# A fourth raw weight buffer in the input projections of a hybrid encoder block

## The chip, the core and the metric

The kernel runs on one core of a Trainium2 chip. The core has five engines with an instruction queue each, every one of them worked off in order: TensorE (PE in the profile, with its weight loads as PEld), VectorE (DVE), ScalarE (ACT), GpSimd (POOL) and SyncE (SP), which here issues the transfers of the weights. The metric is device time in microseconds (us) for one execution; less is better.

## The reference

One block over a sequence of 256 positions and 2048 channels, all in float32. The part that matters here is the first stage:

```python
proj = jnp.einsum('bsd,dc->bsc', h, w_in)            # 2048 -> 12800 columns
lru_x, conv_x, conv_bg, conv_cg, g_lru, g_conv = jnp.split(proj, SPLIT_POINTS, axis=-1)
u = centred_dwconv(lru_x, lru_conv_w, lru_conv_b, LRU_CONV_LEFT)
h_fwd = rg_lru_direction(u, lru_w_a[0], lru_b_a[0], lru_w_x[0], ..., False)   # 20 heads of 128
h_bwd = rg_lru_direction(u, lru_w_a[1], lru_b_a[1], lru_w_x[1], ..., True)
y_lru = jnp.einsum('bsw,wd->bsd', h_fwd + h_bwd, w_lru_out)
v = centred_dwconv(conv_cg * conv_x, sc_conv_w, sc_conv_b, SHORT_CONV_LEFT)
y_conv = jnp.einsum('bsc,cd->bsd', conv_bg * v, w_conv_out)
merged = jax.nn.sigmoid(g_lru) * y_lru + jax.nn.sigmoid(g_conv) * y_conv
h = layer_norm(ALPHA * h + jnp.einsum('bsd,de->bse', merged, w_o), ln1_g, ln1_b)
ff = jnp.square(jax.nn.relu(jnp.einsum('bsd,df->bsf', h, mlp_w1) + mlp_b1))
h = layer_norm(ALPHA * h + jnp.einsum('bsf,fd->bsd', ff, mlp_w2) + mlp_b2, ln2_g, ln2_b)
```

In `rg_lru_direction` each head's `u` goes through two 128x128 gates (sigmoid), and the gates drive a linear recurrence along the sequence (exp, tanh, square root, scan).

## The kernel before

**Precision.** Every operand of a product is kept as a high part and a low part: `hi` is the value cast to the matmul's type, `lo` what the cast left over. For each weight tile `raw` (128 partitions x 1024 values, 512 KB) SP issues the transfer, ACT makes `hi` (L66), DVE makes `lo` (L67). Then PE multiplies: for each of the tile's eight 128x128 blocks one matmul of `hi` with both halves of the input (512 columns, L137) and one of `lo` with the high half (256 columns, L138).

**The stream of weights.** Class `Weights` holds one list of tiles for the whole kernel, in the order in which PE needs them. `load` (L82) takes the next entry: buffers, a transfer, the split. `take` gives a tile to PE's code and makes the loads run five tiles ahead (`AHEAD`). Each kind of buffer is a ring in the pool `wp`: 3 buffers `raw`, 6 `hi`, 6 `lo`. A transfer into a `raw` buffer must wait until DVE has made the `lo` of the tile that had the buffer before, which is the last reader; a cast into a `hi` buffer must wait until PE is done with the tile six places earlier.

**The stages.** In order: the input projections (the tiles below); the 32 gate blocks `sg`; the two output products `yl` and `yc`; `o` with the first norm; the two halves of the MLP, `f` and `d`. The input projections' stage reads 156 tiles: 8 of `b` (the first four column blocks together), then in rounds by head h from 1 to 19: the two tiles of `l{h}` (the recurrent branch's columns), one half-size tile `g{h-1}` (the gate weights of the head before), and two or three `c` blocks of the convolution branch, of two tiles each; then `g19`. This makes 38 tiles of `l`, 90 of `c` and 20 of `g`.

**What comes behind each block.** After an `l` block, `lru_post` adds the two halves of the PSUM bank (`t_l` on ACT, L234; `pad` on DVE, L237), makes the short convolution `u` (four DVE steps, L277 and L279) and splits it into `us` (ACT L66, DVE L67), which the gate's matmuls read (L298 to L300). After the gate, ACT makes four sigmoids (L306). After each second head `recur` handles two heads together: exp and tanh on ACT (L323, L324), products on POOL and DVE (L328, L329), square roots on ACT (L333), scans on DVE (L338, L339); ACT loads another table of functions between them. This burst comes nine times inside the stage.

**What sets the order.** The program is written in job order; a scheduler then sets the order of each engine's queue from priorities and from what it estimates to be ready, with the buffers' waits counted in. So the number of buffers can move instructions. The recurrent branch has a pool of its own, `lp` (L255), open from the start until the first `sg` block is read out; a pool for the gates' results is then opened in its place.

Of the kernel before, what the change touches and what calls it, by code (L numbers as in the profile page):

```python
# [8 lines left out]
F32 = mybir.dt.float32  # L9
# [5 lines left out]
P = 128  # L15
# [11 lines left out]
CH = 8  # L27
# [20 lines left out]
def block_kernel(ctx: ExitStack, tc: tile.TileContext, xT, x, par, w_first, w_in, w_gate, w_lru, w_conv, w_o, w1, w2,  # L48
# [3 lines left out]
    wp = ctx.enter_context(tc.tile_pool(name="wp", bufs=1))  # L52
# [17 lines left out]
    class Weights:  # L70
# [3 lines left out]
            self.specs, self.tiles, self.taken = [], [], 0  # L74

        def alloc(self, name):
            raw = wp.tile([P, CH * P], F32, tag="raw", name=f"raw_{name}", bufs=3)
            hi = wp.tile([P, CH * P], F32R, tag="hi", name=f"hi_{name}", bufs=BUFS)
            lo = wp.tile([P, CH * P], F32R, tag="lo", name=f"lo_{name}", bufs=BUFS)
            return raw, hi, lo  # L80
# [161 lines left out]
    def open_pool(name):  # L242
        scope[name] = es = ExitStack()
        return es.enter_context(tc.tile_pool(name=name, bufs=1, reuse_waits="tile"))
# [10 lines left out]
    lp = open_pool("lru")  # L255
# [337 lines left out]
    src, n, name = stream.specs[0]  # L593
    raw, hi, lo = stream.alloc(name)
# [77 lines left out]
```

## Time and profile before

| | |
|---|---|
| runs | 1645.41 us median of 3 (1641.05 to 1648.22) |
| the profiled execution | 1647.63 us, of which the span from the first to the last instruction is 1645.6 us |
| mean granted TensorE clock | 0.994 |
| PE busy, of the span | 98% |
| DVE, ACT, POOL busy | 64%, 52%, 4% |
| input projections' stage | from the start to 432.9 us, the first `sg` matmul |
| transfers | 312.05 MB, 190 GB/s over the span |

Busy time of PE counts every matmul from its start to its modelled end, and neighbours overlap. So small stops of PE are better found from the starts of successive matmuls, and from the idle time that the profile prints with the instruction that came late, than from the busy share. In the trace's lists of instructions the columns are: start, duration (us), engine, line, operation, what it writes and reads, how many; and in brackets the idle time of the engine before it and what ended that.

### The profile page before, as it was taken

What the parts mean: (1) busy time and instruction counts of PE and PEld (TensorE: products, weight loads), DVE (VectorE), ACT (ScalarE), POOL (GpSimd) and SP (SyncE); (2) the same over time, 40 slices, a digit from 0 to 9 for tenths busy, and PEclk for the clock granted to TensorE, in tenths of its full rate; (3) what the DMA queues carried; (4) which work ended last, traced back from release to release, by engine and by line L of the source; (5) the groups of instructions that cost most, each with busy time, mean ns of one, the idle gap of its engine ahead of it and who ended that gap; (6) DMA issues with size and microseconds to landing.
All of it is one profiled execution on the core that took longest, in us unless ns stands there. A gap on an engine that the chain in (4) does not pass through costs nothing.

```text
span 1645.6 us, 22702 instructions
## 1 busy us (share of the span) xinstructions
PE 1616.0 (98%) x8592; PEld 1377.5 (84%) x8592; DVE 1060.3 (64%) x1435; ACT 849.1 (52%) x1216; POOL 62.2 (4%) x69
## 2 busy tenths in 40 slices
PE   8999999999999999999999899999999999999997
PEld 7888888888888888888888788888888888888885
DVE  6788898888865546666555687654444666655444
ACT  5777676677755444444343545543333444543331
POOL 0111111111100000000000000000000000000001
PEclk9999999999999999999999899999999999999999
DMA  7555555555565555655774455555555555565552
GB/s 252 169 179 192 181 178 186 186 170 189 186 206 205 191 177 188 190 188 185 249 257 159 152 188 203 189 186 190 186 186 190 187 186 191 188 235 192 184 186 102
DMA packets 88364, 312.05 MB, mean 190 GB/s; under 512 B 9792, under 2 KB 10176, under 8 KB 87360
## 3 DMA queue, kind: packets, MB, share of 16 engines
q1 hardware_dynamic: 86976, 302.75, 54.9%
q0 software_dynamic: 992, 7.34, 1.2%
q8 instruction: 67, 1.10, 0.3%
q10 hardware_dynamic: 288, 0.52, 0.1%
q14 instruction: 41, 0.34, 0.1%
HBM read 308.48 MB, written 2.10 MB: 189 GB/s over the span
## 4 chain that ended last, share of the span: by engine, by line
PE 80%; DVE 6%; DMA 6%; ACT 4%; issue 3%; POOL 0%; SPq 0%; POOLq 0%; ACTq 0%; DVEq 0%
PE ps_f L137 15%; PE ps_f L138 7%; PE pr_d L208 7%; PE pr_d L206 7%; PE pr_d L207 7%; PE ps_sg L137 7%; PE ps_yl L137 5%; PE ps_sg L138 4%; PE ps_yc L137 4%; PE ps_c L137 4%; DMA raw_l<-in_w_in 2%; PE ps_yl L138 2%; DMA raw_c<-in_w_in 2%; PE ps_c L138 2%; PE ps_yc L138 2%
## 5 line engine op out<-in xcount | busy, mean ns | idle before, releaser
L137 PE MATMUL ps_f<-hsp,hi_f 128*128 128x512 f32 x1024 | 360.6, 395 | 0.9 <-DVE hsp L478 0.9
L138 PE MATMUL ps_f<-hsp,lo_f 128*128 128x256 f32 x1024 | 286.6, 280 | 0.0
L67 DVE TENSOR_TENSOR lo_d<-raw_d,hi_d 128x1024 fp32r<-128x1024 f32 x128 | 156.7, 1225 | 183.7 <-ACT hi_d L66 183.7
L137 PE MATMUL ps_c<-xs,hi_c 128*128 128x512 f32 x720 | 254.8, 395 | 0.0
L66 ACT CAST hi_d<-raw_d 128x1024 fp32r<-128x1024 f32 x128 | 134.6, 1052 | 214.8 <-PE pr_d L208 192.6
L137 PEld LDWEIGHTS ps_f<-hsp,hi_f 128*128 128x128 f32 x1024 | 192.9, 188 | 47.6 <-ACT hf L474 1.2
L67 DVE TENSOR_TENSOR lo_f<-raw_f,hi_f 128x1024 fp32r<-128x1024 f32 x128 | 156.4, 1225 | 117.8 <-ACT hi_f L66 117.0
L66 ACT CAST hi_f<-raw_f 128x1024 fp32r<-128x1024 f32 x128 | 134.5, 1052 | 176.3 <-PE ps_f L137 143.8
L138 PE MATMUL ps_c<-xs,lo_c 128*128 128x256 f32 x720 | 202.6, 281 | 4.7 <-DVE lo_c L67 4.6
L208 PE MATMUL pr_d<-hi_d,ff 128*128 128x512 f32 x512 | 203.0, 396 | 0.0
L206 PE MATMUL pr_d<-hi_d,ff 128*128 128x512 f32 x512 | 203.0, 396 | 0.0
L207 PE MATMUL pr_d<-lo_d,ff 128*128 128x512 f32 x512 | 203.0, 396 | 0.0
L138 PEld LDWEIGHTS ps_f<-hsp,lo_f 128*128 128x128 f32 x1024 | 192.9, 188 | 0.0
L137 PE MATMUL ps_sg<-xs,hi_sg 128*128 128x512 f32 x512 | 179.3, 393 | 0.0
L137 PEld LDWEIGHTS ps_c<-xs,hi_c 128*128 128x128 f32 x720 | 135.7, 188 | 31.3
L138 PE MATMUL ps_sg<-xs,lo_sg 128*128 128x256 f32 x512 | 142.9, 279 | 0.0
L138 PEld LDWEIGHTS ps_c<-xs,lo_c 128*128 128x128 f32 x720 | 135.6, 188 | 7.6 <-DVE lo_c L67 7.6
L67 DVE TENSOR_TENSOR lo_c<-raw_c,hi_c 128x1024 fp32r<-128x1024 f32 x90 | 111.9, 1244 | 26.2 <-ACT hi_c L66 25.9
L66 ACT CAST hi_c<-raw_c 128x1024 fp32r<-128x1024 f32 x90 | 94.3, 1048 | 64.6 <-DMA raw_c<-in_w_in 60.4
L67 DVE TENSOR_TENSOR lo_sg<-raw_sg,hi_sg 128x1024 fp32r<-128x1024 f32 x64 | 78.9, 1232 | 68.1 <-ACT hi_sg L66 66.2
L208 PEld LDWEIGHTS pr_d<-hi_d,ff 128*128 128x128 f32 x512 | 96.4, 188 | 23.5
L206 PEld LDWEIGHTS pr_d<-hi_d,ff 128*128 128x128 f32 x512 | 96.4, 188 | 23.5
(168 smaller groups left out, 2804.0 us busy)
## 6 DMA issues: line engine op xcount, KB each, us to landing
raw_f<-in_w SPq DMA_DIRECT2D x128, 512.0 KB, 4.7
raw_d<-in_w SPq DMA_DIRECT2D x128, 512.0 KB, 4.3
raw_c<-in_w_in SPq DMA_DIRECT2D x90, 512.0 KB, 3.9
raw_sg<-in_w_in SPq DMA_DIRECT2D x64, 512.0 KB, 4.0
raw_l<-in_w_in SPq DMA_DIRECT2D x38, 512.0 KB, 4.6
raw_yl<-in_w_lru SPq DMA_DIRECT2D x32, 512.0 KB, 4.2
raw_yc<-in_w_conv SPq DMA_DIRECT2D x32, 512.0 KB, 3.7
raw_o<-in_w_o SPq DMA_DIRECT2D x32, 512.0 KB, 4.2
```

The source lines that it names most:

```text
L66: made = nc.scalar.copy(hi, raw)
L67: nc.vector.tensor_tensor(lo, raw, hi.bitcast(F32), op=ALU.subtract)
L137: nc.tensor.matmul(ps, hi[:, w], s, start=i == 0, stop=False)
L138: nc.tensor.matmul(ps[:, :T], lo[:, w], s[:, :T], start=False, stop=i == n - 1)
L206: nc.tensor.matmul(ps[t], sh, hi[:, c], start=k == 0, stop=False)
L207: nc.tensor.matmul(ps[t], sh, lo[:, c], start=False, stop=False)
L208: nc.tensor.matmul(ps[t], sl, hi[:, c], start=False, stop=k == nk - 1)
```

## The change

In the input projections' stage every tile whose number in the stream leaves 3 when divided by 4 gets its `raw` from a new buffer `raw4` (4 KB in each partition) in the pool `lp`, in place of one of the three of the ring in `wp`. Only tiles named `c`, `l` or `g` are meant, so tiles 11, 15, 19 and so on up to 155, which is `g19`; the eight `b` tiles and all tiles from `sg` on keep the ring of three. The names of the numbered tiles in the program's lists leave out the number of the head or part: `raw_l_8` is the second tile of an `l` block, `raw_c_1_0` the first tile of a convolution block of column group 1.

```diff
         def alloc(self, name):
-            raw = wp.tile([P, CH * P], F32, tag="raw", name=f"raw_{name}", bufs=3)
+            i = len(self.tiles)
+            if name[0] in "clg" and i % 4 == 3:
+                raw = lp.tile([P, CH * P], F32, tag="raw4", name=f"raw_{name}")
+            else:
+                raw = wp.tile([P, CH * P], F32, tag="raw", name=f"raw_{name}", bufs=3)
             hi = wp.tile([P, CH * P], F32R, tag="hi", name=f"hi_{name}", bufs=BUFS)
             lo = wp.tile([P, CH * P], F32R, tag="lo", name=f"lo_{name}", bufs=BUFS)
             return raw, hi, lo
```

No instruction is added or removed, and PE's and POOL's queues keep their order. The queues of SP, ACT and DVE change in places. Lines after L77 stand four lines later in the changed kernel. SP's queue at the start, where the transfers of the first `c` and `l` blocks follow the last `b` tiles, before:

```order
L85 DMA raw_b_199<-in_w_first 128x1024
L85 DMA raw_c_1_0_221<-in_w_in 128x1024
L85 DMA raw_c_1_8_243<-in_w_in 128x1024
L85 DMA raw_l_0_265<-in_w_in 128x1024
L85 DMA raw_l_8_287<-in_w_in 128x1024
L85 DMA raw_g_309<-in_w_gate 128x512
```

and with the change:

```order
L89 DMA raw_b_199<-in_w_first 128x1024
L89 DMA raw_c_1_0_221<-in_w_in 128x1024
L89 DMA raw_l_8_287<-in_w_in 128x1024
L89 DMA raw_c_1_8_243<-in_w_in 128x1024
L89 DMA raw_l_0_265<-in_w_in 128x1024
L89 DMA raw_g_309<-in_w_gate 128x512
```

The transfer of tile 11, the first with the new buffer, has moved past two others. ACT's queue a little later, up to the cast `us` that gate 0 waits for, before:

```order
L66 CAST hi_g_310<-raw_g_309 128x512
L66 CAST hi_c_1_0_333<-raw_c_1_0_332 128x1024
L234 COPY t_cx_476<-ps_c_1_331 128x256
L66 CAST hi_c_1_8_355<-raw_c_1_8_354 128x1024
L66 CAST us_384<-u_379 128x256
```

and with the change:

```order
L66 CAST hi_g_310<-raw_g_309 128x512
L238 COPY t_cg_415<-ps_b_159 128x256
L238 COPY t_cb_424<-ps_b_160 128x256
L66 CAST hi_c_1_0_333<-raw_c_1_0_332 128x1024
L66 CAST hi_c_1_8_355<-raw_c_1_8_354 128x1024
L238 COPY t_cx_476<-ps_c_1_331 128x256
L66 CAST hi_c_1_0_432<-raw_c_1_0_431 128x1024
L66 CAST us_384<-u_379 128x256
```

One more weight cast, `hi_c_1_0_432`, now stands ahead of `us`; the two copies `t_cg` and `t_cb` stood ahead of `hi_g` before. ACT's queue at the end of the stage, where gate 19 waits for its `us`, before:

```order
L66 CAST hi_g_4405<-raw_g_4404 128x512
L306 ACTIVATE ri_4426<-pg_1_4357,par_sb 128x256
L234 COPY t_cx_4478<-ps_c_15_4381 128x256
L66 CAST hi_sg_0_4434<-raw_sg_0_4433 128x1024
L66 CAST us_4378<-u_4373 128x256
```

and with the change:

```order
L310 ACTIVATE ri_4426<-pg_1_4357,par_sb 128x256 x2
L66 CAST hi_sg_0_4434<-raw_sg_0_4433 128x1024
L238 COPY t_cx_4478<-ps_c_15_4381 128x256
L66 CAST hi_sg_8_4456<-raw_sg_8_4455 128x1024
L66 CAST us_4378<-u_4373 128x256
```

Here, too, one more weight cast, `hi_sg_8_4456`, stands ahead of `us`; on DVE the matching `lo_sg_8` stands ahead of the low part of `us`.

## The prediction

> **What bounds the kernel now.** I read the page's busy times first, then the table of stretches, then PE's waits, and last the waits of the engines that feed it.
>
> ```profile
> span 1645.6 us, 22702 instructions
> PE 1616.0 (98%) x8592; PEld 1377.5 (84%) x8592; DVE 1060.3 (64%) x1435; ACT 849.1 (52%) x1216; POOL 62.2 (4%) x69
> ```
>
> PE is busy 98% of the span: nothing but its stops can be won, and the change touches only those of the first 433 us. How long PE would need there without stops follows from the starts of its matmuls where nothing stops it:
>
> ```profile
> 36.01 0.39 PE L137 MATMUL ps_l<-xs,hi_l 128*128 128x512 f32 x1
> 38.81 0.39 PE L137 MATMUL ps_l<-xs,hi_l 128*128 128x512 f32 x1
> ...
> 64.02 0.28 PE L298 MATMUL pg<-us,hi_g 128*128 128x256 f32 x1
> 65.44 0.40 PE L137 MATMUL ps_c<-xs,hi_c 128*128 128x512 f32 x1
> 68.25 0.39 PE L137 MATMUL ps_c<-xs,hi_c 128*128 128x512 f32 x1
> ...
> 45.96:432.89 386.93, 379.42 (x2214) 331.08 (x2214) 330.27 (x506) 277.42 (x452) 46.37 (x37) 1.00 0.54 180
> ```
>
> A gate takes 1.42 us (64.02 to 65.44), a full tile 2.80 (to 68.25, rounded down). From 45.96, the first matmul of tile 13, to 432.89, the first of `sg`, PE works off 143 tiles: 19 gates and 124 others, 19 x 1.42 + 124 x 2.80 = 374.2 us. It took 386.9, so 12.7 us are lost. Ahead of it, the second `l` tile and gate 0 took from 38.81 to 45.96, 7.15 us for 4.2: 2.9 lost. **The stage holds 15.6 us of stops, 0.95% of the span.** What they wait for:
>
> ```profile
> PEld ps_c L138 <- DVE lo_c L67: 7.6, 10, 1.6
> PEld pg L299 <- DVE us L67: 3.5, 4, 1.1
> PEld pg L298 <- ACT us L66: 3.2, 3, 1.5
> ...
> 42.95 0.19 PEld L298 LDWEIGHTS pg<-us,hi_g 128*128 128x128 f32 x1 [1.50 <-ACT us L66]
> 44.24 0.19 PEld L299 LDWEIGHTS pg<-us,hi_g 128*128 128x128 f32 x1 [1.10 <-DVE us L67]
> 430.19 0.19 PEld L298 LDWEIGHTS pg<-us,hi_g 128*128 128x128 f32 x1 [1.19 <-ACT us L66]
> 431.48 0.19 PEld L299 LDWEIGHTS pg<-us,hi_g 128*128 128x128 f32 x1 [1.10 <-DVE us L67]
> ```
>
> The first three rows are all the waits of 38.81 to 432.89 (us, times, longest): ten late `lo_c` tiles, 7.6 us; late `us` of four gates, 6.7 us. Of these, gate 0 has 2.6 (the rows at 43 and 44), gate 19 has 2.3 (430 and 431), and gates 9 and 15 the remaining 1.8. About 1.5 more is a slow clock behind gate 0:
>
> ```profile
> 46.00:50.00 4.00, 4.00 (x17) 3.42 (x17) 2.65 (x10) 3.97 (x7) 0.00 (x0) 0.67 0.55 193
> 46.16 0.43 PE ps_c L137
> 48.08 0.43 PE ps_c L137
> ```
>
> The granted clock was 0.67 there, and three pairs of matmuls took 1.92 us (46.16 to 48.08), 0.64 each for 0.35 otherwise. Together 7.6 + 6.7 + 1.5 = 15.8, the 15.6 within rounding.
>
> **Why the tiles are late.** These rows are the loop of a `raw` buffer: transfer, cast, subtraction, and SP's wait for it.
>
> ```profile
> raw_c<-in_w_in SPq DMA_DIRECT2D x90, 512.0 KB, 3.9
> raw_l<-in_w_in SPq DMA_DIRECT2D x38, 512.0 KB, 4.6
> L67 DVE TENSOR_TENSOR lo_c<-raw_c,hi_c 128x1024 fp32r<-128x1024 f32 x90 | 111.9, 1244 | 26.2 <-ACT hi_c L66 25.9
> L66 ACT CAST hi_c<-raw_c 128x1024 fp32r<-128x1024 f32 x90 | 94.3, 1048 | 64.6 <-DMA raw_c<-in_w_in 60.4
> ...
> SPq L85 <- DVE lo_c L67: 104.7, 42, 4.4
> ACT hi_c L66 <- DMA raw_c<-in_w_in: 57.7, 42, 2.9
> ACT hi_l L66 <- DMA raw_l<-in_w_in: 23.9, 17, 3.5
> DVE lo_c L67 <- ACT hi_c L66: 23.5, 32, 2.1
> DVE lo_l L67 <- ACT hi_l L66: 13.1, 14, 2.1
> ```
>
> Landing 3.9 to 4.6 us, cast 1.05, `lo` 1.24: 6.2 to 6.9 us if no engine queue is in the way. Three buffers give PE 3 x 2.80 = 8.4 us of work per turn, so a delay of 1.5 to 2.2 us in ACT's or DVE's queue already makes feeding slower than PE. The last rows show it: SP waits 105 us for `lo_c` alone, ACT idles 81.6 us for transfers, DVE 36.6 for casts. The tiles run dry where the recurrence's burst holds both engines:
>
> ```profile
> 194.81 1.23 DVE L67 TENSOR_TENSOR lo_l<-raw_l,hi_l 128x1024 fp32r<-128x1024 f32 x1 [0.52 <-ACT hi_l L66]
> 200.46 0.39 PE L137 MATMUL ps_l<-xs,hi_l 128*128 128x512 f32 x1
> 205.55 1.04 ACT L66 CAST hi_c<-raw_c 128x1024 fp32r<-128x1024 f32 x1
> 207.53 1.20 DVE L67 TENSOR_TENSOR lo_c<-raw_c,hi_c 128x1024 fp32r<-128x1024 f32 x1
> 208.78 0.19 PEld L138 LDWEIGHTS ps_c<-xs,lo_c 128*128 128x128 f32 x1 [1.23 <-DVE lo_c L67]
> 290.26 0.19 PEld L138 LDWEIGHTS ps_c<-xs,lo_c 128*128 128x128 f32 x1 [1.59 <-DVE lo_c L67]
> ```
>
> The `l` tile's `lo` ended at 196.04 and PE began the tile at 200.46, 4.4 us ahead; two full tiles and a gate later PE waits 1.23. The burst eats 5.6 us of lead, and what stands before it is less. The deepest shortfall of the stage is the 1.59 at 290.
>
> **The change, part by part.**
>
> *Four buffers in turn.* Tile 4n+3 has its own buffer and the ring of three takes the others, so each transfer waits for the `lo` four tiles back, not three: 4 x 2.80 = 11.2 us of PE work per turn against 6.2 to 6.9. What is late next is the cast's `hi` buffer, six tiles deep, and the queues of ACT and DVE. They can give the lead: per burst (nine) ACT idles 9 us for transfers and DVE 4 for casts; 1.6 more lead is enough at the worst place. The bound below is no gain, the bound above 7.6. I take the end that the idle rows are nearer to, and leave 1.0 for places where the queues alone are late: **6.6 us**.
>
> *Gates 9 and 15.* Their `us` stood in ACT's and DVE's queue behind casts without lead; the same lead covers them. Between 0 and 1.8, I take **1.6**.
>
> *Gate 0, the start.* Now ACT idles for the cast ahead of `us`:
>
> ```profile
> 0.00:35.00 35.00, 30.08 (x155) 25.73 (x156) 19.59 (x23) 19.44 (x26) 0.53 (x12) 1.00 0.73 253
> 25.55 6.18 DMA raw_l<-in_w_in
> 41.55 1.04 ACT L66 CAST hi_c<-raw_c 128x1024 fp32r<-128x1024 f32 x1 [2.30 <-DMA raw_c<-in_w_in]
> 42.50 0.40 ACT L66 CAST us<-u 128x256 fp32r<-128x256 f32 x1
> ```
>
> With the change `us` stands behind one more cast (1.05 us on ACT), but the transfers of these `c` tiles are released one tile earlier. `raw_l_8` moves past `raw_c_1_8` and `raw_l_0` on SP's queue; it waits for no buffer, so it holds up neither there, only on the wire. At the stretch's 253 GB/s its 0.52 MB are 2.1 us of transfer. Both ends: all 2.6 and the 1.5 of slow clock saved, or none saved and 1.05 more. The 2.30 us of ACT's idle is nearest; I take a rest of 1.2: **2.9**.
>
> The Trainium skill's "TensorE: Matmul & The Clock Gate" (What's actually happening) says that the clock halves after an idle window of about 3.4 us and comes back after as long a busy one. The trace agrees with the half (0.64 for 0.35) but shows it behind two stops of 1.50 and 1.10 us with work between, and not behind the single stops at 208 and 290. If the slow clock does not hang on these stops, as that rule read strictly would have it, the sum is 1.5 smaller.
>
> *Gate 19, the end.* ACT idles for the first `sg` transfer ahead of `us`:
>
> ```profile
> 428.78 1.05 ACT L66 CAST hi_sg<-raw_sg 128x1024 fp32r<-128x1024 f32 x1 [3.75 <-DMA raw_sg<-in_w_in]
> 429.74 0.40 ACT L66 CAST us<-u 128x256 fp32r<-128x256 f32 x1
> ```
>
> Gate 19 is tile 155 and so leaves the ring: each of the first three `sg` transfers is released one tile earlier. Against that `us` now waits for two `sg` casts, one transfer and 1.05 us more. Between 2.3 saved and 2.8 lost (a tile's turn); the 3.75 us of idle and the lead of the first term speak for a saving, the added cast against all of it: **1.3**.
>
> *The rest.* No engine has more to do, and casts moved ahead of PSUM copies have a bank three blocks of slack. After 433 us the queues are in the old order and PE is the bound, so what it gains arrives at the end:
>
> ```profile
> 660.00:900.00 240.00, 240.00 (x1247) 203.33 (x1246) 140.82 (x182) 100.56 (x128) 3.58 (x8) 1.00 0.63 208
> ```
>
> Here PE is busy throughout at clock 1.00, so a denser first stage gives no reason for a lower clock.
>
> Sum: 6.6 + 1.6 + 2.9 + 1.3 = 12.4 us. The profiled execution took 1647.6 us (span 1645.6 and 2.0 around it), 2.2 above the median of 1645.4; the change makes it 1635.2, and the median **1633.0**.
>
> **The rivals.**
>
> *The burst, not the ring.* The cast at 205.55 had no idle time ahead: its transfer had landed, and ACT and DVE were busy with the recurrence. If lead cannot be stored before a burst, the 7.6 stay, and the gates and the start give 2 to 6: 1639.4 to 1643.4. Against it speak the 81.6 us that ACT idled between bursts. Chance 0.20.
>
> *No effect.* DVE is busy 330 of 387 us; if the stage is bound by it, each stop comes back elsewhere: 1643.4 to 1645.4. DVE's idle for casts, 36.6 us, speaks against. Chance 0.08.
>
> *Slower: the early transfer of `raw_l_8`.* If it goes in full ahead of `raw_c_1_8` and `raw_l_0`, these land up to 2.1 us later. `raw_l_0` landed at 31.73; with cast and `lo` it was ready at 34.13, and PE began it at 36.01: 1.9 of lead. It decides from there on: some 0.2 us of stop, up to 1.0 with `pad` and `cx`, now ahead of its `lo`, and a second slow stretch like the 1.5; with 1.05 more at gate 0 and 2.8 at gate 19, and nothing gained, 6.4: 1651.8. The Trainium skill's "DMA: Bandwidth & Descriptors" (Queues, rings and completion order) has descriptors of one ring consumed in order, which is this rival's mechanism; no row of before shows two transfers in another order. Against it: the 1.9 us of lead cover nearly the whole of one transfer. Chance 0.04.
>
> **How the numbers follow.** Forecast 0.68: a gain of 9.0 to 15.6, 1629.8 to 1636.4. A measurement tells about 0.5% from no change, 8.2 us: faster is the forecast, 0.68; the first two rivals are the same, 0.28; slower takes the last, 0.04, though its price worked out here lies just inside the bound. Range: all stops gone is 1629.8, less 1.8 for the spread of runs (1641 to 1648), 1628; above, most of the first rival, 1643.
>
> **What would show it.** Right: the ten waits of `ps_c` for `lo_c` fall below 1 us in all; ACT's idle for `raw_c` at least halves; the first `sg` matmul starts near 420.5; the clock of 46 to 50 us is 1.00. Wrong: waits for `lo_c` remain after each burst with ACT busy (first rival), PE stops at `ps_l` near 36 (third), or gates wait for `us` longer than now.

## The result, and the profile after

| | before | with the change |
|---|---|---|
| median | 1645.29 us of 6 runs (1641.05 to 1648.22) | 1632.58 us of 6 runs (1630.77 to 1633.24) |
| ratio | | 0.9919, 95% interval 0.9905 to 0.9933 |
| profiled execution | 1647.63 us, span 1645.6 | 1631.94 us, span 1629.8 |
| first `sg` matmul | 432.89 us | 417.71 us |

The kernel is 12.7 us faster by the medians and 15.7 us by the two profiled executions. From the first `sg` matmul to the end both profiles need nearly the same: 1645.6 - 432.9 = 1212.7 us before, 1629.8 - 417.7 = 1212.1 now. So the gain lies in the input projections' stage, as seen in the profile's head, in the stretches of the changed kernel (window, length, busy us of PE, PEld, DVE, ACT and POOL with counts, then the granted clock, the transfers' share and GB/s) and in the start of `sg`:

```profile
span 1629.8 us, 22722 instructions
PE 1607.2 (99%) x8592; PEld 1372.8 (84%) x8592; DVE 1058.4 (65%) x1435; ACT 846.2 (52%) x1216; POOL 65.3 (4%) x69
```

```profile
46.00:50.00 4.00, 4.00 (x25) 3.50 (x24) 3.69 (x13) 3.97 (x7) 0.00 (x0) 1.00 0.36 132
39.00:417.71 378.71, 378.71 (x2244) 334.08 (x2243) 336.86 (x520) 281.41 (x464) 48.70 (x37) 1.00 0.57 189
```

```profile
417.71 0.40 PE L141 MATMUL ps_sg<-xs,hi_sg 128*128 128x512 f32 x1
```

The head counts 20 instructions more than before, but the working instructions of each engine are the same in number; the 20 are not among them.

PE is busy from 39 us to the end of the stage without a stop, and the granted clock at 46 to 50 us is 1.00 where it was 0.67. All waits of PE's weight loads in the whole execution, a list that before began with 7.6 us for `lo_c`:

```profile
PEld ps_b L141 <- ACT hi_b L66: 5.5, 2, 4.9
PEld tr L473 <- DVE z L459: 4.1, 1, 4.1
PEld ps_f L141 <- ACT hf L478: 2.7, 1, 2.7
PEld ps_b L142 <- DVE lo_b L67: 1.5, 2, 1.1
```

Neither `lo_c` nor `us` is in it; what is left are the first tiles and the first norm. The waits of ACT and DVE in the same stretch (us, times, longest):

```profile
ACT hi_c L66 <- PE ps_l L141: 12.9, 11, 1.7
ACT hi_l L66 <- PE ps_l L141: 12.2, 8, 1.8
ACT hi_c L66 <- PE ps_c L141: 10.5, 10, 1.8
ACT hi_c L66 <- DMA raw_c<-in_w_in: 9.9, 5, 2.8
...
DVE lo_c L67 <- ACT hi_c L66: 16.2, 20, 1.6
DVE lo_l L67 <- ACT hi_l L66: 8.6, 8, 1.6
```

ACT waited 57.7 us for `raw_c` and 23.9 for `raw_l`; now it waits 9.9 for `raw_c`, and 0.5 for `raw_l`. Instead it waits for PE to give back a `hi` buffer, 35.6 us in the first three rows: the casts have caught up as far as the ring of six lets them. The lowest lead after a burst:

```profile
76.54 1.20 DVE L67 TENSOR_TENSOR lo_c<-raw_c,hi_c 128x1024 fp32r<-128x1024 f32 x1
...
82.78 0.39 PE L141 MATMUL ps_c<-xs,hi_c 128*128 128x512 f32 x1
```

This `lo` ends at 77.74 and PE begins the tile at 82.78, 5.0 us later; this is the first burst, and behind the others the lowest lead is 5.5 us or more. With three buffers the worst tile came 1.6 us too late.

### The profile page after: what moved, and what is told of

The parts are those of the page before. It is cut to its first block, busy times and chain, and to the rows that moved or that the text cites. A ratio compares the mean times of both kernels' runs of the same rounds, so it can differ in the third digit from the quotient of the medians.

```text
span 1629.8 us, 22722 instructions
## 1 busy us (share of the span) xinstructions
PE 1607.2 (99%) x8592; PEld 1372.8 (84%) x8592; DVE 1058.4 (65%) x1435; ACT 846.2 (52%) x1216; POOL 65.3 (4%) x69
## 4 chain that ended last, share of the span: by engine, by line
PE 98%; DVE 1%; issue 1%; DMA 0%; POOL 0%; SPq 0%; ACT 0%; POOLq 0%
PE ps_f L141 15%; PE ps_c L141 10%; PE ps_f L142 7%; PE pr_d L212 7%; PE pr_d L210 7%; PE pr_d L211 7%; PE ps_sg L141 7%; PE ps_c L142 5%; PE ps_yl L141 5%; PE ps_l L141 4%; PE ps_sg L142 4%; PE ps_yc L141 4%; PE ps_yl L142 2%; PE ps_l L142 2%; PE ps_yc L142 2%; PE pr_o L212 2%
## 5 line engine op out<-in xcount | busy, mean ns | idle before, releaser
L211 PEld LDWEIGHTS pr_d<-lo_d,ff 128*128 128x128 f32 x512 | 96.4, 188 | 23.4
```

The costliest lines, as they stand in the source:

```text
L211: nc.tensor.matmul(ps[t], sh, lo[:, c], start=False, stop=False)
```

## Experiments

Theory A is the prediction's: the recurrence's bursts use up the lead, and with three `raw` buffers the feed is too slow to build it up again. Rival B: not the number of buffers, but the queues' new order or the buffer's place. Rival C: the start alone decides. Diffs are against the changed kernel unless said otherwise. A stage's length is read from the first `sg` matmul.

### Three buffers, one of them in the recurrent branch's pool

```diff
-            if name[0] in "clg" and i % 4 == 3:
+            if name[0] in "clg" and i % 3 == 2:
                 raw = lp.tile(..., tag="raw4", ...)
             else:
-                raw = wp.tile(..., tag="raw", ..., bufs=3)
+                raw = wp.tile(..., tag=f"raw{i % 3}", ...)
```

> Three raw buffers as before, but every third tile of the stage has its buffer in the recurrent branch's pool. Theory A (the number of buffers lets lead be stored ahead of the bursts): the turn is 3 x 2.80 = 8.4 us as before, so late lo_c tiles and late us remain, 10 to 12 us of stops in PE's weight loads, about 1645 us; only the start may change by 1 to 2 us, since one transfer there goes early. Rival B (the place of the buffer, or the transfer that the scheduler draws to the start, does it): about 1633 us and no stops.

Measured: 1646.20 us of 10 runs, ratio 1.001 (0.9999 to 1.0021). The waits of PE's weight loads from 38 to 434 us, and the stretch behind gate 0:

```profile
PEld ps_c L142 <- DVE lo_c L67: 13.0, 15, 1.7
PEld pg L303 <- DVE us L67: 2.3, 4, 0.9
PEld pg L302 <- ACT us L66: 0.4, 2, 0.2
```

```profile
46.00:50.00 4.00, 4.00 (x25) 3.49 (x24) 3.32 (x7) 3.97 (x7) 0.00 (x0) 1.00 0.38 132
...
433.38 0.39 PE L141 MATMUL ps_sg<-xs,hi_sg 128*128 128x512 f32 x1
```

Neither the pool nor a transfer drawn to the start (here one of an `sg` tile, issued at 21.29 us) makes the kernel faster; the place half of rival B falls. The run shows something that nobody had expected, too. Gate 0's two long stops and the slow clock are gone here (clock 1.00), 4 us of the prediction's terms, and yet the stage ends at 433.4 as before, because ten tiles' wait of 7.6 us became fifteen tiles' of 13.0. The leads tell why: a stop of PE is also time in which the feed gets ahead. The tile behind gate 0 was ready 5.7 us before PE began it in the kernel before, which had stopped there, and 3.1 us here. **With three buffers the stage is bound by its feed: a stop that is taken away at one place comes back at another.**

### The fourth buffer from tile 27 on

```diff
-            if name[0] in "clg" and i % 4 == 3:
+            if name[0] in "clg" and i % 4 == 3 and i > 24:
```

> The fourth buffer only from tile 27 on; the ring of three up to there. Theory A: gate 0's stops (2.6 us) and the slow clock behind them (1.5) come back, the ten late lo_c tiles and gates 9, 15 and 19 stay cured: 4 us over the changed kernel, about 1637 us. Rival C (the start decides the lead of the whole stage): stops after the bursts come back, 1643 to 1645 us.

Measured: 1633.93 us of 4 runs, ratio 0.9935 (0.9919 to 0.9951). The first `sg` matmul starts at 420.31. All waits from 38 us to the end of the stage lie at the first burst (80 and 85 us):

```profile
PEld ps_c L142 <- DVE lo_c L67: 2.2, 2, 1.7
PEld pg L303 <- DVE us L67: 0.2, 1, 0.2
```

Theory A's expectation of 4 us over the changed kernel was too much: it is 1.4 us by the medians and 2.6 by the first `sg` matmul, and for another reason. Gate 0 doesn't stop, though it has only three buffers. The queue tells why: the first transfer into `raw4` is again drawn to the start, the scheduler reorders what follows, and `us` now stands directly behind the first of the `c` casts:

```profile
37.92 1.05 ACT L66 CAST hi_c<-raw_c 128x1024 fp32r<-128x1024 f32 x1 [2.07 <-DMA raw_c<-in_w_in]
38.87 0.40 ACT L66 CAST us<-u 128x256 fp32r<-128x256 f32 x1
```

Before, `us` was made at 42.50, behind a second `c` cast that had waited for its transfer. So here a change of order alone cures gate 0's stop. What three buffers up to tile 26 cost is the first burst, 2.2 us, where the kernel before, with more lead from its stop at gate 0, had no stop; rival C falls for the bursts behind it.

### The fourth buffer only at the start

```diff
-            if name[0] in "clg" and i % 4 == 3:
+            if name[0] in "clg" and i % 4 == 3 and i < 24:
```

> The fourth buffer only for tiles 11, 15, 19 and 23. Theory A: gate 0 runs without stops (4 us saved), the lead gained is used up by the first one or two bursts, and the late lo_c tiles from 208 us on remain, 9 to 12 us: about 1641 us. Rival C (the start decides): about 1633 us and hardly a late tile.

Measured: 1639.68 us of 10 runs, ratio 0.9973 (0.9963 to 0.9982). From 61 us on, ahead of the first burst, ACT's and DVE's instructions follow one another by name as in the kernel before, and the ring has three buffers. The lead of the first burst's second tile, and the first wait for `lo_c` behind it:

```profile
76.59 1.20 DVE L67 TENSOR_TENSOR lo_c<-raw_c,hi_c 128x1024 fp32r<-128x1024 f32 x1
...
82.72 0.39 PE L141 MATMUL ps_c<-xs,hi_c 128*128 128x512 f32 x1
...
282.72 0.19 PEld L142 LDWEIGHTS ps_c<-xs,lo_c 128*128 128x128 f32 x1 [0.93 <-DVE lo_c L67]
```

4.9 us of lead at 77.8 (where the kernel before had 1.0) carried five bursts without a stop, three of which had stopped PE in the kernel before; I had expected one or two. The lowest leads behind them were 4.9, 3.0, 2.9, 2.1 and 1.9 us: each burst takes a little more than the ring of three brings back. Only the sixth burst, at 282.7 us, used it up. From there on PE waits 8.4 us in all. The five bursts passed with the queues' old order and three buffers, by lead alone. This speaks against the order half of rival B, and C falls again: lead from the start isn't enough.

### Five tiles between two bursts

```diff
-            if name[0] in "clg" and i % 4 == 3:
+            if name[0] in "clg" and i % 4 == 3 and 80 <= i < 100:
```

> The fourth buffer only for the tiles 83, 87, 91, 95 and 99, between two bursts, where ACT's and DVE's queues keep their old order but for one copy; from tile 100 on all is as in the kernel before. Theory A: the lead grows there by 2 us or more over the kernel before, so the burst at tiles 103 and 104, which had stops of 1.0 and 1.6 us, passes with none, and later bursts stop again as the lead decays. If the new order of the queues does it, the stops at tiles 103 and 104 stay.

One run, 1643.54 us. PE's weight loads wait 6.7 us for `lo_c` in 7 places before 260 us:

```profile
PEld ps_c L142 <- DVE lo_c L67: 6.7, 7, 1.7
PEld pg L303 <- DVE us L67: 0.6, 2, 0.4
```

Between 260 and 350 us there is no wait at all, where the kernel before had stops at 285, 290, 333, 339, 348 and 349. The two bursts there passed with leads of 2.6 and 1.0 us at their worst tiles; the next ones, at 374 and 412 us, stop again. Theory A's expectation held, with the old order of the queues: behind 70 us only one cast of ACT stands elsewhere by name.

### The fourth buffer for every eighth tile

```diff
-            if name[0] in "clg" and i % 4 == 3:
+            if name[0] in "clg" and i % 8 == 3:
```

> The fourth buffer for every eighth tile, so that half of the transfers wait for the lo three tiles back and half for the lo four back: 9.8 us of PE work in a turn on the mean. Theory A: the lead at its lowest after a burst lies between that of three (-1.6 us) and that of four buffers (5 us or more), some 1 to 3 us; nearly all stops are gone, 0 to 3 us of them left, 1633 to 1636 us. If a turn must hold a full fourth buffer each time, the lead doesn't build up and 8 or more us of stops remain, 1641 us or more.

Measured: 1632.26 us of 4 runs, ratio 0.9929 (0.9910 to 0.9949), no wait for `lo_c` behind the start, 0.7 us at gate 0. The lowest lead after a burst:

```profile
160.84 1.20 DVE L67 TENSOR_TENSOR lo_c<-raw_c,hi_c 128x1024 fp32r<-128x1024 f32 x1
...
162.26 0.39 PE L141 MATMUL ps_c<-xs,hi_c 128*128 128x512 f32 x1
```

It is 0.2 us, less than the 1 to 3 that I had expected. In time a turn of 9.8 us on the mean is as good as one of 11.2, but only just. What a turn lacked at 8.4 was small.

### Two buffers

```diff
-            if name[0] in "clg" and i % 4 == 3:
-                raw = lp.tile(..., tag="raw4", ...)
-            else:
-                raw = wp.tile(..., tag="raw", ..., bufs=3)
+            k = i % 2 if name[0] in "clg" else i % 3
+            raw = wp.tile(..., tag=f"raw{k}", ...)
```

> Two raw buffers in the input projections' stage, three elsewhere. Theory A: a turn of two tiles is 5.6 us of PE work and the loop of a buffer takes 6.2 to 6.9 us without delays, so that the stage is bound by the loop throughout: at least 0.3 to 0.65 us on each of some 120 full tiles and more at the bursts, 60 to 110 us longer in all, 1705 to 1755 us, with DVE idle for casts in every turn. If the loop is shorter than its rows say (a cast doesn't wait out the transfer), 20 to 50 us longer.

One run, 1714.13 us. PE waits in more than ninety places of the stage, most of all:

```profile
PEld ps_c L140 <- DVE lo_c L67: 45.6, 51, 1.8
PEld ps_c L139 <- ACT hi_c L66: 12.9, 16, 1.9
PEld ps_l L140 <- DVE lo_l L67: 11.7, 15, 1.6
...
45.57 0.39 PE L139 MATMUL ps_c<-xs,hi_c 128*128 128x512 f32 x1
...
45.00:495.00 450.00, 401.82 (x2202) 332.72 (x2201) 336.90 (x505) 281.20 (x450) 52.43 (x37) 0.99 0.46 155
```

From 45.57 to the first `sg` matmul at 498.86 it took 453.3 us for the 143 tiles that need 374.2 without stops. Without the 19 gates (27 us) that is 3.44 us a tile, 6.9 for a turn of two, more than the 5.6 us of work that a turn gives PE: the stage is bound by the loop. The 6.9 is also the upper end of the loop that the prediction had added up, 6.2 to 6.9, but this agreement is in part chance. Transfers land in 3.6 to 3.7 us in this run (medians of `raw_l` and `raw_c`), which makes the loop 5.9 us without delays, and the 6.9 holds the bursts and the engines' queues as well.

### Three buffers without the bursts

Against the kernel before; the recurrence is left out, and the gated input stands in for its result:

```diff
     def recur(hh, last):
-        ...
+        for h in hh:
+            ri = heads[h]["ri"]
+            d = hsrc(h)
+            split(ri[:, 2, :], d[:, :T], d[:, T:])
```

> The kernel before, with three raw buffers, and the recurrence left out (no exp, tanh, square root, products and scans; the gated input takes the place of the recurrence's result). Theory A (the bursts of the recurrence use up the lead, and three buffers can't refill it between them): the late lo_c tiles (7.6 us) and the late us of gates 9, 15 and 19 (4.1) vanish, only gate 0's stop may stay: about 1633 us. If the ring of three is too slow for PE by itself, burst or not, stops of 8 us and more remain, 1641 us or more.

Measured: 1631.42 us of 4 runs, ratio 0.9922 (0.9901 to 0.9943), first `sg` matmul at 417.84. One wait is left from 20 us on:

```profile
PEld pg L299 <- DVE us L67: 0.6, 1, 0.6
```

The stretch 45.96 to 417 us here and, below it, in the changed kernel:

```profile
45.96:417.00 371.04, 371.04 (x2193) 326.95 (x2192) 288.26 (x421) 204.55 (x337) 24.54 (x19) 1.00 0.58 191
45.96:417.00 371.04, 371.04 (x2194) 327.13 (x2193) 330.67 (x510) 274.17 (x452) 48.70 (x37) 1.00 0.56 188
```

Three buffers are enough for PE if nothing breaks the feed, and four are enough with the bursts. The stops needed both, the recurrence and the short ring. This run takes away the recurrence's whole work on DVE and ACT (42 and 70 us in the stretch), its mean as well as its coming in bursts; that it is the bursts is read from where the lead falls, which the runs with lead at the start and between two bursts show.

### Five `hi` and `lo` buffers

```diff
-BUFS = 6
+BUFS = 5
```

> The changed kernel with rings of five hi and lo buffers for six. Theory A: the lead is capped one tile (2.8 us) lower, and the lowest lead after a burst, 5.5 us with the change, falls to about 2.7: still no stops in the input projections, the first sg matmul near 418 us; the other stages may lose some us at the norm, where tiles cast ahead cover a pause: 1633 to 1638 us. If the depth of hi and lo is what holds the lead at the bursts, stops come back: 1640 us or more.

Measured: 1634.17 us of 4 runs, ratio 0.9931 (0.9912 to 0.9950), and no wait between 20 and 440 us. The lowest lead after a burst:

```profile
317.89 1.20 DVE L67 TENSOR_TENSOR lo_c<-raw_c,hi_c 128x1024 fp32r<-128x1024 f32 x1
...
321.35 0.40 PE L141 MATMUL ps_c<-xs,hi_c 128*128 128x512 f32 x1
```

It is 2.3 us, near the 2.7 expected. The next ring isn't short.

### Four `raw` and five `hi` and `lo` for the whole kernel

```diff
-AHEAD = 5
-BUFS = 6
+AHEAD = 4
+BUFS = 5
...
-            if name[0] in "clg" and i % 4 == 3:
-                raw = lp.tile(..., tag="raw4", ...)
-            else:
-                raw = wp.tile(..., tag="raw", ..., bufs=3)
+            raw = wp.tile(..., tag="raw", ..., bufs=4)
```

(The first loads of the input are split otherwise, so that they still cover all of it.)

> A ring of four raw buffers for the whole kernel, in the common pool, and rings of five hi and lo buffers for six, with loads that run four tiles ahead for five: 4 KB a partition less than the kernel before. Theory A: only the input projections' stage lacked raw buffers, and five hi and lo were enough there, so the time is that of the changed kernel, 1631 to 1636 us, with no stops for lo_c and no further gain in later stages, where PE stops only at the norm. If a fourth raw buffer also helps later stages, 1630 us or less; if the lead of four tiles is too short, stops come back, 1640 us.

Measured: 1632.91 us of 4 runs, ratio 0.9931 (0.9913 to 0.9949). The time is that of the changed kernel, with 4 KB a partition less than the kernel before and no special case. No gain of later stages from a fourth buffer shows; the `hi` and `lo` buffers and the number of tiles that the loads run ahead were changed with it.

### The first tiles as well

```diff
-            if name[0] in "clg" and i % 4 == 3:
+            if name[0] in "bclg" and i % 4 == 3:
```

> As the changed kernel, and the first eight tiles take the fourth buffer too (tiles 3 and 7). PE stops some 1.5 us at 10 to 11 us with the change, for the second tile. Theory A: in these first 20 us the transfers share nearly full DMA engines (share 0.8 to 0.9), so another buffer only makes them share earlier: 1632 to 1634 us, stops at 10 us between 0.5 and 3 us. If the ring of three is what limits the start as well, these stops go: 1631 us.

Measured: 1631.00 us of 4 runs, ratio 0.9918 (0.9902 to 0.9934), not to be told from the changed kernel's 0.9919. PE still waits at 10 to 11 us:

```profile
10.45 0.29 PEld L141 LDWEIGHTS ps_b<-xs,hi_b 128*128 128x128 f32 x1 [0.26 <-ACT hi_b L66]
11.71 0.19 PEld L142 LDWEIGHTS ps_b<-xs,lo_b 128*128 128x128 f32 x1 [0.97 <-DVE lo_b L67]
...
4.00:11.00 7.00, 6.09 (x17) 4.55 (x17) 2.96 (x5) 3.75 (x6) 0.00 (x0) 1.00 0.99 307
```

The share of the transfers (the number before the last) is 0.99 of all sixteen engines in that stretch. In that stretch the transfers fill the DMA engines, and a fourth buffer does not shorten it.

## Why the prediction was right, and where it wasn't

*Four buffers in turn: 6.6 forecast, 7.6 in the profile.* The mechanism held in every step that was put to the test: the loop as the bound of a short ring (two buffers), lead that is stored ahead of a burst (the start alone, and the five tiles), the bursts as what uses it up (three buffers without them). I had left 1.0 for places where the queues alone are late; there are none, since the lead stays at 5.0 us or more behind every burst.

*Gates 9 and 15: 1.6 forecast, 1.8. Gate 19: 1.3 forecast, 2.3.* These are the same lead. The added cast ahead of gate 19's `us`, for which I had taken off 1.0, costs nothing: with lead, both `sg` casts are done long before PE needs `us`.

*Gate 0: 2.9 forecast of 4.1, all gone.* The reason that I gave shows in the changed kernel, and the size was wrong. ACT's queue there:

```profile
34.65 1.05 ACT L66 CAST hi_c<-raw_c 128x1024 fp32r<-128x1024 f32 x1 [0.90 <-DMA raw_c<-in_w_in]
38.18 1.05 ACT L66 CAST hi_c<-raw_c 128x1024 fp32r<-128x1024 f32 x1 [2.47 <-DMA raw_c<-in_w_in]
39.61 1.05 ACT L66 CAST hi_c<-raw_c 128x1024 fp32r<-128x1024 f32 x1
40.92 0.41 ACT L66 CAST us<-u 128x256 fp32r<-128x256 f32 x1 [0.26 <-DVE u L283]
```

The transfers came earlier (SP issues the first of these `c` tiles at 30.89 us, before at 34.16), so `us` is made 1.6 us earlier than the 42.50 of before, although one more cast stands ahead of it. The added cast, for which I had kept a rest of 1.2, costs nothing: behind it `us` still waits 0.26 us for `u`. But earlier transfers are not the only cure. In the run with three buffers and in the run with the fourth from tile 27 on, these transfers are issued at 34.62 and 34.04 us, about as late as before, and another order of ACT's queue takes the stop away. And by itself this saves nothing, as the run with three buffers shows.

*The sum.* What failed is that the terms were added as if each stood for itself. With three buffers they are one budget: curing 4 us of stops at gate 0 brought 5.4 more for `lo_c`, against 1.4 less for the other gates' `us`. They all go together once the feed is faster than PE, which a turn of 9.8 us just is. So the gain is the whole of the stage's stops, the end of the range that I had called its lower bound, 15.6, and not 12.4: the profiled executions differ by 15.7. (Of these the stage's end shows 15.2; the changed kernel begins the second `l` tile 0.5 us later, at 39.3 us.)

*The median.* 1633.0 was forecast, 1632.58 measured, closer than the steps deserve; that is luck. The profiled execution of before was 2.3 us above its median and that of the change 0.6 below, so the medians differ by 12.7 and not by 15.7. The runs of before scatter over 7.2 us and those of the change over 2.5. That the stops differ from run to run would explain both, but only one execution of before was profiled, so this stays open.

*The rivals.* "The burst, not the ring" had the right cause and the wrong conclusion: lead can be stored, and the rows of ACT's idle time between bursts that spoke against it were the right ones to weigh. "No effect": DVE is busy 336.9 of 378.7 us in the stage now and PE doesn't stop, so DVE wasn't the bound. "Slower": PE doesn't stop at the first `l` tiles, where no wait is listed between 20 us and the end of the stage. The first `sg` matmul was forecast near 420.5 and came at 417.7.

*The clock.* The slow stretch at 46 us went with the stops at gate 0. I had set this behind two stops with work between, against the single stops at 208 and 290. But gate 19 had two such stops, of 1.19 and 1.10 us, and the clock stayed at 1.00 there. What sets the two gates apart is in the last section.

## What to carry to other kernels

Count a ring in time: buffers times what the consumer takes for one, against the loop of transfer, conversion and hand-back with its rows' durations. Where it holds only just (8.4 against 6.2 to 6.9 here), every burst on the converting engines takes lead that isn't fully refilled, and the sign is an engine that idles for transfers between bursts and is late in them. In a stage that is bound by its feed don't add up single stops; what is cured at one place comes back at the next until the feed itself is faster, and then all of them go.

## What the hardware did that I had not expected

The granted clock of TensorE halved behind stops far shorter than the slow stretch itself. In the kernel before it stood at 0.50 from 45.23 to 48.64 us, 3.41 us, behind stops of 1.50 and 1.10 us. In the kernel with two buffers PE stopped more than ninety times, up to 1.9 us. The clock's mean over 45 to 495 us was 0.99, but it fell to 0.50 for 3.41 us three times in that stretch, and once more at its end. The four begin at 166.19, 217.39, 360.75 and 500.69 us, which is 15, 42 and 41 times 3.413 us apart: slow stretches begin and end on a grid of such steps. Cut along that grid, the kernel before at gates 0 and 19:

```profile
41.81:45.23 3.42, 1.37 (x9) 1.18 (x10) 2.61 (x5) 3.37 (x6) 0.00 (x0) 1.00 0.44 152
45.23:48.64 3.41, 3.41 (x14) 3.02 (x14) 2.06 (x7) 3.37 (x7) 0.00 (x0) 0.50 0.76 252
427.52:430.93 3.41, 2.17 (x12) 1.48 (x10) 2.20 (x4) 2.15 (x3) 0.00 (x0) 1.00 0.66 210
430.93:434.35 3.42, 2.87 (x20) 2.68 (x21) 2.90 (x5) 1.53 (x3) 0.00 (x0) 1.00 0.56 196
```

and the kernel with two buffers, at the busiest step that a slow one followed and at the idlest that none followed:

```profile
497.28:500.69 3.41, 1.62 (x9) 1.05 (x8) 2.65 (x5) 3.30 (x7) 0.00 (x0) 1.00 0.28 114
500.69:504.11 3.42, 3.42 (x13) 2.94 (x12) 2.12 (x2) 3.39 (x6) 1.77 (x1) 0.50 0.75 232
111.57:114.98 3.41, 1.82 (x13) 1.30 (x11) 2.71 (x5) 3.13 (x6) 0.00 (x0) 1.00 0.16 61
114.98:118.40 3.42, 3.13 (x18) 2.77 (x19) 3.20 (x4) 3.39 (x7) 2.14 (x1) 1.00 0.50 174
```

So in this stage every step of 3.41 us in which PE was busy 1.62 us or less was followed by one at half the clock (five of five), and in no run was one with 1.82 us or more. The two stops of gate 0 fell almost whole into one step; the second one of gate 19 was cut by a step's edge. How much PE works within a step, and not the length of a single stop, tells these cases apart. The bound is not sharp everywhere: at the first norm of the changed kernel two steps with 1.5 and 1.6 us of busy time, from 889.5 to 896.3 us, kept the full clock.
